# Contrast adjustment on one core: tiles of one size against tiles of two sizes in the same ring

## The chip, the core and the metric

The kernel runs on one core of a Trainium2 chip. Time is device time of that core in microseconds (us). The engines that matter here are VectorE (DVE in the profile), ScalarE (ACT), TensorE (PE, with PEld for its weight loads), GpSimd (POOL) and SyncE (SP). Transfers between the chip's main memory (DRAM) and the core's on-chip memory (SBUF, 128 partitions) are done by 16 DMA engines. They are fed from two hardware queues here: q1 holds what SP issues, which are all the loads, and q10 holds what ACT issues, which are all the stores.

## The reference

```python
def reference(x, factor):          # x: 16 x 3 x 512 x 512 float32, factor 1.5
    mean = np.mean(x, axis=(2, 3), keepdims=True)
    return np.clip(mean + factor * (x - mean), 0, 1).astype(np.float32)
```

There are 48 images (16 times 3) of 262,144 values each. Each image needs its own mean before its first output can be computed. With w = (1 - factor) / 262144, an output is clip(factor * x + w * sum(image), 0, 1). 50.33 MB come in and 50.33 MB go out.

## The kernel before

**Tiles.** The images are cut into rows of ROW = 8192 floats (32 KB), so an image is 32 rows. A tile is 128 rows, one per partition: four images, 4 MB. There are 12 tiles. They live in `ring` (L66), six slots of 32 KB per partition; tile t uses slot t % 6.

**Loads** (`load`, L68, issued on SP at L76). The order is written by hand (L103 to L112, a manual schedule: each engine's instructions run in program order, and the semaphores between engines follow from the data). Tile 0 is loaded in two pieces, 2048 columns and 6144 columns. Tile 1 is one load. Tiles 2 and 3 come in one load of 8 MB, tiles 4 and 5 in another. After `compute(t)` the load of tile t + 6 follows on SP; it waits until tile t has been stored, since it takes its slot.

**Compute** (`compute`, L78). VectorE sums columns 0 to SUM = 4352 of the tile per row (L81), while ScalarE sums the other 3840 columns with an accumulating copy into `junk` (L84). Two accumulating matmuls with `blockw` (L86 on ScalarE's sums, L87 on VectorE's) add the 32 rows of each image, multiply by w and put the result into every row of the image, in PSUM (`bias`). `blockw` is a 128 x 128 block diagonal matrix with 32 x 32 blocks of w, filled by GpSimd (L61, L63). Then VectorE makes two passes over the tile in place: multiply by factor and add the shift (L91), and clip (L94). ACT issues the store (L101). Tile 0 does this in two parts (`FIRST`, 2048 and 6144 columns), each with a store of its own. The other tiles do it in one.

**Queues.** On ACT the order is: sum of tile t, store of tile t, sum of tile t + 1, and so on. On VectorE: sum, pass, pass of tile t, then those of tile t + 1. On SP: the loads alone.

Of the kernel before, what the change touches and what calls it, by code (L numbers as in the profile page):

```python
# [1 line left out]

# [4 lines left out]


P = 128  # L10
ROW = 8192
BUFS = 6
SHORT = 2048
FIRST = (SHORT, ROW - SHORT)
SUM = 4352


@with_exitstack
def kernel(
    ctx: ExitStack,  # L20
    tc: tile.TileContext,
    x: bass.AP,
    factor: float,
    out: bass.AP,
):

    nc = tc.nc
    f32 = mybir.dt.float32  # L30
    Alu = mybir.AluOpType
    Act = mybir.ActivationFunctionType

    B, C, H, W = x.shape
    n_img, n_pix = B * C, H * W
    ppi = n_pix // ROW
    per_tile = P // ppi
    n_tiles = n_img // per_tile
    assert ppi * ROW == n_pix and per_tile * n_tiles == n_img

    factor = float(factor)
    wconst = (1.0 - factor) / float(n_pix)

    x_f = x.rearrange("b c h w -> (b c h w)")
    out_f = out.rearrange("b c h w -> (b c h w)")

    def dram(ap, t, c0=0, c1=ROW):
        return bass.AP(tensor=ap.tensor, offset=t * P * ROW + c0, ap=[[ROW, P], [1, c1 - c0]])

    consts = ctx.enter_context(tc.tile_pool(name="consts", bufs=1))  # L50
    xpool = ctx.enter_context(tc.tile_pool(name="xpool", bufs=1))
    small = ctx.enter_context(tc.tile_pool(name="small", bufs=1))
    psum = ctx.enter_context(tc.tile_pool(name="psum", bufs=1, space=bass.MemoryType.PSUM))


    sums = small.tile([P, 2 * n_tiles], f32, name="sums")
    junk = small.tile([P, ROW - SUM], f32, name="junk")
    bias = psum.tile([P, n_tiles], f32, name="bias")

    blockw = consts.tile([P, P], f32, name="blockw")  # L60
    nc.gpsimd.memset(blockw, 0.0)  # L61
    for a in range(0, P, ppi):
        nc.gpsimd.memset(blockw[a : a + ppi, a : a + ppi], wconst)  # L63


    ring = xpool.tile([P, BUFS, ROW], f32, name="ring")  # L66

    def load(t, c0=0, c1=ROW, n=1):  # L68

        b = t % BUFS  # L70
        src = bass.AP(
            tensor=x_f.tensor,
            offset=t * P * ROW + c0,
            ap=[[ROW, P], [P * ROW, n], [1, c1 - c0]],
        )
        nc.sync.dma_start(out=ring[:, b : b + n, c0:c1], in_=src)  # L76

    def compute(t):  # L78
        xt = ring[:, t % BUFS, :]
        own = sums[:, 2 * t : 2 * t + 2]  # L80
        nc.vector.tensor_reduce(  # L81
            out=own[:, 0:1], in_=xt[:, 0:SUM], axis=mybir.AxisListType.X, op=Alu.add
        )
        nc.scalar.activation(out=junk, in_=xt[:, SUM:ROW], func=Act.Copy, accum_out=own[:, 1:2])  # L84
        shift = bias[:, t : t + 1]
        nc.tensor.matmul(shift, blockw, own[:, 1:2], start=True, stop=False)  # L86
        nc.tensor.matmul(shift, blockw, own[:, 0:1], start=False, stop=True)  # L87
        c = 0
        for n in FIRST if t == 0 else [ROW]:
            part = xt[:, c : c + n]  # L90
            nc.vector.tensor_scalar(  # L91
                out=part, in0=part, scalar1=factor, scalar2=shift, op0=Alu.mult, op1=Alu.add
            )
            nc.vector.tensor_scalar(  # L94
                out=part, in0=part, scalar1=0.0, scalar2=1.0, op0=Alu.max, op1=Alu.min
            )
            store(t, c, c + n)
            c += n

    def store(t, c0, c1):  # L100
        nc.scalar.dma_start(out=dram(out_f, t, c0, c1), in_=ring[:, t % BUFS, c0:c1])  # L101

    with tc.manual_schedule():  # L103
        load(0, c1=SHORT)
        load(0, c0=SHORT)
        load(1)
        load(2, n=2)
        load(4, n=2)
        for t in range(n_tiles):
            compute(t)  # L110
            if t + BUFS < n_tiles:
                load(t + BUFS)  # L112


# [1 line left out]
_INS = ['x', 'factor']  # L116
_OUTS = [((16, 3, 512, 512), 'float32')]

_NUMBERS = {'factor': 1.5}


# [26 lines left out]
```

## Time and profile before

| what | value |
|---|---|
| median of 3 runs | 239.26 us (239.2 to 239.46) |
| span of the profiled execution | 237.3 us, 285 instructions |
| around the span, by the median | 2.0 us (the page gives the profiled execution no time of its own beside its span) |
| busy: DVE / ACT / PE | 163.1 (69%) / 43.2 (18%) / 14.1 (6%) us |
| moved | 100.66 MB, mean 424 GB/s over the span |
| transfers | 11 loads, 13 stores; all of 4 MB but two loads of 8 MB and the two pieces of tile 0 |
| time from the last load's landing to the last store's issue | 203.73 to 218.17 us |

The page divides the span into 40 slices of 5.93 us; a row of digits shows how busy an engine was in each, in tenths. A DMA share is the busy time of all 16 DMA engines as a share of 16 times the stretch, so share x 16 x stretch / packets is the mean time of one packet on its engine. A packet here is one contiguous piece of one partition's row: a 4 MB transfer is 128 packets of 32 KB, eight on each DMA engine. Very small packets (4 bytes) are the semaphore updates, 16 for each transfer. Shares a little over 100% come from packets that reach over the edge of the stretch.

### The profile page before, as it was taken

How to read it: one execution, taken by the hardware profiler on the slowest of the kernel's cores; microseconds unless marked ns; L12 is line 12 of the kernel's file. 1: busy time of each engine (PE TensorE's matmuls, PEld its weight loads, DVE VectorE, ACT ScalarE, POOL GpSimd, SP SyncE). 2: the span in 40 equal slices, each digit the busy share in tenths (PEclk: the TensorE clock that was granted, in tenths of full speed). 3: DMA queues.
4: the chain of work that ended last, by engine and by line, in shares of the span. 5: the costliest groups of instructions: out<-in, count | busy, mean ns of one | idle time of the engine just before them, and what ended most of it. 6: DMA issues, size and time to landing. Idle time of an engine off the chain costs nothing.

```text
span 237.3 us, 285 instructions
## 1 busy us (share of the span) xinstructions
PE 14.1 (6%) x48; PEld 12.0 (5%) x48; DVE 163.1 (69%) x38; ACT 43.2 (18%) x25; POOL 0.9 (0%) x9
## 2 busy tenths in 40 slices
PE   0010010001010001010010100100100100010000
PEld 0010010001010001010010100100100100010000
DVE  0079989048989328999989898891892795687000
ACT  2050230041050023050320504101400500500000
POOL 1000000000000000000000000000000000000000
DMA  7999999999999999999999999999999999999996
GB/s 297 410 442 442 421 442 359 456 439 441 442 436 414 403 431 442 442 442 442 436 442 436 414 409 425 442 442 442 442 436 442 436 420 403 425 442 442 442 442 265
DMA packets 3712, 100.66 MB, mean 424 GB/s; under 512 B 384, under 2 KB 384, under 8 KB 384
## 3 DMA queue, kind: packets, MB, share of 16 engines
q1 hardware_dynamic: 1840, 50.33, 49.7%
q10 hardware_dynamic: 1872, 50.33, 49.2%
HBM read 50.33 MB, written 50.33 MB: 424 GB/s over the span
## 4 chain that ended last, share of the span: by engine, by line
DMA 57%; DVE 29%; another core or an unknown queue 3%; PE 1%; SPq 1%; issue 0%; DVEq 0%
DMA ring<-in_x_dram 41%; DMA out_dram<-ring 16%; DVE sums L81 10%; DVE ring L91 9%; DVE ring L94 9%; PE bias L87 1%; SPq L76 1%; DVEq L91 0%
## 5 line engine op out<-in xcount | busy, mean ns | idle before, releaser
L81 DVE TENSOR_REDUCE sums<-ring 128x1 f32<-128x4352 f32 x12 | 56.2, 4683 | 45.7 <-DMA ring<-in_x_dram 45.7
L84 ACT ACTIVATE junk<-ring 128x3840 f32<-128x3840 f32 x12 | 40.8, 3403 | 163.3 <-DMA ring<-in_x_dram 107.5
L91 DVE TENSOR_SCALAR ring<-ring,bias 128x8192 f32<-128x8192 f32 (+2 forms) x13 | 54.1, 4163 | 8.9 <-PE bias L87 7.4
L94 DVE TENSOR_SCALAR ring<-ring 128x8192 f32<-128x8192 f32 (+2 forms) x13 | 53.3, 4099 | 0.4
L86 PE MATMUL bias<-sums,blockw 128*128 128x1 f32 x24 | 7.0, 361 | 190.8 <-ACT junk L84 190.8
L86 PEld LDWEIGHTS bias<-sums,blockw 128*128 128x128 f32 x24 | 6.0, 312 | 191.7 <-ACT junk L84 175.2
L87 PE MATMUL bias<-sums,blockw 128*128 128x1 f32 x24 | 7.0, 363 | 4.3 <-DVE sums L81 3.9
L87 PEld LDWEIGHTS bias<-sums,blockw 128*128 128x128 f32 x24 | 6.0, 311 | 5.3 <-DVE sums L81 5.0
L84 ACT ACTIVATION_READ_ACCUMULATOR junk<-ring 128x1 f32 x12 | 2.2, 186 | 0.0
L84 ACT ACT_TABLE_LOAD x1 | 1.3, 1283 | 0.7 <-PEq L129 0.7
L63 POOL MEMSET blockw<- 32x32 f32 x4 | 0.5, 117 | 0.2
L61 POOL MEMSET blockw<- 128x128 f32 x1 | 0.2, 204 | 0.3 <-POOLq L129 0.3
L129 POOL MEMSET const-bfloat16-1.0<- 128x1 bf16 x1 | 0.1, 111 | 0.0
L129 POOL MEMSET const-uint8-127<- 128x1 uint8 x1 | 0.1, 111 | 0.0
L129 POOL MEMSET const-float32-1.0<- 128x1 f32 x1 | 0.1, 108 | 0.0
L129 POOL MEMSET const-float32-0.0<- 128x1 f32 x1 | 0.1, 103 | 0.2 <-issue 0.2
## 6 DMA issues: line engine op xcount, KB each, us to landing
out_dram<-ring ACTq DMA_DIRECT2D x11, 4096.0 KB, 35.8
ring<-in_x_dram SPq DMA_DIRECT2D x7, 4096.0 KB, 49.7
ring<-in_x_dram SPq DMA_DIRECT2D x2, 8192.0 KB, 66.7
ring<-in_x_dram SPq DMA_DIRECT2D x1, 3072.0 KB, 11.7
out_dram<-ring ACTq DMA_DIRECT2D x1, 3072.0 KB, 28.2
ring<-in_x_dram SPq DMA_DIRECT2D x1, 1024.0 KB, 4.8
out_dram<-ring ACTq DMA_DIRECT2D x1, 1024.0 KB, 17.5
```

The lines of the kernel that those rows point to most:

```text
L61: nc.gpsimd.memset(blockw, 0.0)
L63: nc.gpsimd.memset(blockw[a : a + ppi, a : a + ppi], wconst)
L76: nc.sync.dma_start(out=ring[:, b : b + n, c0:c1], in_=src)
L81: nc.vector.tensor_reduce(out=own[:, 0:1], in_=xt[:, 0:SUM], axis=mybir.AxisListType.X, op=Alu.add)
L84: nc.scalar.activation(out=junk, in_=xt[:, SUM:ROW], func=Act.Copy, accum_out=own[:, 1:2])
L86: nc.tensor.matmul(shift, blockw, own[:, 1:2], start=True, stop=False)
L87: nc.tensor.matmul(shift, blockw, own[:, 0:1], start=False, stop=True)
L91: nc.vector.tensor_scalar(out=part, in0=part, scalar1=factor, scalar2=shift, op0=Alu.mult, op1=Alu.add)
L94: nc.vector.tensor_scalar(out=part, in0=part, scalar1=0.0, scalar2=1.0, op0=Alu.max, op1=Alu.min)
L129: nc = _bacc.Bacc("TRN2", target_bir_lowering=False, num_devices=1)
```

## The change

The ring stays 192 KB per partition, now as six units of 32 KB (`SLOTS`, `UNIT`). A list `PLAN` gives each tile its first unit and its width in units. Eight tiles replace twelve: tiles 0 and 1 of four images (one unit each, units 0 and 1), tiles 2 to 5 of eight images (two units each), tiles 6 and 7 of four images (units 4 and 5). In a tile of eight images a partition holds one contiguous row of 16384 floats (64 KB), so an image is 16 rows. In the DRAM tensors the rows of such a tile are 64 KB apart.

- Loads: tile 0 in two pieces as before, then tiles 1, 2, 3 without a wait. Tile 4 goes to units 0 and 1 and waits for the stores of tiles 0 and 1. Tile 5 goes to units 2 and 3 and waits for the store of tile 2. Tiles 6 and 7 go to units 4 and 5 and wait for the store of tile 3. There are 9 loads and 9 stores (tile 0 has two of each).
- Sums: VectorE takes VEC = 4480 columns per unit of width in one instruction (8960 in a wide tile); ScalarE takes 3712 columns per unit, in one instruction for a narrow tile and in two for a wide one. A wide tile has a matmul for each of ScalarE's two sums and one for VectorE's.
- The two passes over a wide tile are each one instruction over 16384 columns, and its store is one transfer of 8 MB.
- GpSimd makes two block matrices (16 x 16 and 32 x 32 blocks), each with a memset and two `affine_select` in place of the memsets of single blocks.

```diff
-ROW = 8192
-BUFS = 6
+UNIT = 8192
+SLOTS = 6
 SHORT = 2048
-SUM = 4352
+VEC = 4480
+PLAN = ((0, 1), (1, 1), (2, 2), (4, 2), (0, 2), (2, 2), (4, 1), (5, 1))
...
+    def dram(ap, t, c0, c1):
+        row = UNIT * PLAN[t][1]
+        return bass.AP(tensor=ap.tensor, offset=start[t] + c0, ap=[[row, P], [1, c1 - c0]])
...
-    blockw = consts.tile([P, P], f32, name="blockw")
-    nc.gpsimd.memset(blockw, 0.0)
-    for a in range(0, P, ppi):
-        nc.gpsimd.memset(blockw[a : a + ppi, a : a + ppi], wconst)
+    for w in sorted({w for _, w in PLAN}):
+        rows = n_pix // (UNIT * w)
+        m = consts.tile([P, P], f32, name=f"block{w}")
+        nc.gpsimd.memset(m, wconst)
...
+    def load(t, c0=0, c1=None):
+        c1 = UNIT * PLAN[t][1] if c1 is None else c1
+        nc.sync.dma_start(out=cols(t, c0, c1), in_=dram(x_f, t, c0, c1))
...
         nc.vector.tensor_reduce(
-            out=own[:, 0:1], in_=xt[:, 0:SUM], axis=mybir.AxisListType.X, op=Alu.add
+            out=own[:, 0:1], in_=cols(t, 0, VEC * w), axis=mybir.AxisListType.X, op=Alu.add
         )
-        nc.scalar.activation(out=junk, in_=xt[:, SUM:ROW], func=Act.Copy, accum_out=own[:, 1:2])
+        for i in range(w):
+            a = VEC * w + i * (UNIT - VEC)
+            nc.scalar.activation(
+                out=junk, in_=cols(t, a, a + UNIT - VEC), func=Act.Copy,
+                accum_out=own[:, 1 + i : 2 + i],
+            )
...
+    held, after = {}, {}
+    for t, (s, w) in enumerate(PLAN):
+        before = [held[k] for k in range(s, s + w) if k in held]
+        after.setdefault(max(before, default=-1), []).append(t)
+        held.update({k: t for k in range(s, s + w)})
 
     with tc.manual_schedule():
-        load(0, c1=SHORT)
-        load(0, c0=SHORT)
-        load(1)
-        load(2, n=2)
-        load(4, n=2)
-        for t in range(n_tiles):
+        load(0, 0, SHORT)
+        load(0, SHORT)
+        for t in after[-1][1:]:
+            load(t)
+        for t in range(len(PLAN)):
             compute(t)
-            if t + BUFS < n_tiles:
-                load(t + BUFS)
+            for n in after.get(t, ()):
+                load(n)
```

More of the change, by code (lines that the diff above doesn't have):

```diff
@@ L10 @@
 P = 128
-ROW = 8192
-BUFS = 6
+UNIT = 8192
+SLOTS = 6
 SHORT = 2048
-FIRST = (SHORT, ROW - SHORT)
-SUM = 4352
+VEC = 4480
+PLAN = ((0, 1), (1, 1), (2, 2), (4, 2), (0, 2), (2, 2), (4, 1), (5, 1))
 @with_exitstack
@@ L34 @@
     B, C, H, W = x.shape
[L35 to L39, printed above, removed]
+    n_pix = H * W
+    assert P * UNIT * sum(w for _, w in PLAN) == B * C * n_pix
     factor = float(factor)
@@ L45 @@
     out_f = out.rearrange("b c h w -> (b c h w)")
-    def dram(ap, t, c0=0, c1=ROW):
-        return bass.AP(tensor=ap.tensor, offset=t * P * ROW + c0, ap=[[ROW, P], [1, c1 - c0]])
+    start, begin = [], 0
+    for _, w in PLAN:
+        start.append(begin)
+        begin += P * UNIT * w
+    def dram(ap, t, c0, c1):
+        row = UNIT * PLAN[t][1]
+        return bass.AP(tensor=ap.tensor, offset=start[t] + c0, ap=[[row, P], [1, c1 - c0]])
     consts = ctx.enter_context(tc.tile_pool(name="consts", bufs=1))
@@ L53 @@
     psum = ctx.enter_context(tc.tile_pool(name="psum", bufs=1, space=bass.MemoryType.PSUM))
-    sums = small.tile([P, 2 * n_tiles], f32, name="sums")
-    junk = small.tile([P, ROW - SUM], f32, name="junk")
-    bias = psum.tile([P, n_tiles], f32, name="bias")
-    blockw = consts.tile([P, P], f32, name="blockw")
-    nc.gpsimd.memset(blockw, 0.0)
-    for a in range(0, P, ppi):
-        nc.gpsimd.memset(blockw[a : a + ppi, a : a + ppi], wconst)
-    ring = xpool.tile([P, BUFS, ROW], f32, name="ring")
@@ L68, in load @@
[L68 to L74, printed above, removed]
-        )
-        nc.sync.dma_start(out=ring[:, b : b + n, c0:c1], in_=src)
+    sums = small.tile([P, 3 * len(PLAN)], f32, name="sums")
+    junk = small.tile([P, UNIT - VEC], f32, name="junk")
+    bias = psum.tile([P, len(PLAN)], f32, name="bias")
+    block = {}
+    for w in sorted({w for _, w in PLAN}):
+        rows = n_pix // (UNIT * w)
+        m = consts.tile([P, P], f32, name=f"block{w}")
+        nc.gpsimd.memset(m, wconst)
+        v = m.rearrange("p (g j) -> p g j", j=rows)
+        nc.gpsimd.affine_select(
+            out=v, in_=v, pattern=[[-rows, P // rows], [0, rows]], compare_op=Alu.is_ge,
+            fill=0.0, base=0, channel_multiplier=1,
+        )
+        nc.gpsimd.affine_select(
+            out=v, in_=v, pattern=[[rows, P // rows], [0, rows]], compare_op=Alu.is_ge,
+            fill=0.0, base=rows - 1, channel_multiplier=-1,
+        )
+        block[w] = m
@@ L78, in compute, with cols, store @@
+    ring = xpool.tile([P, SLOTS * UNIT], f32, name="ring")
+    def cols(t, c0, c1):
+        a = PLAN[t][0] * UNIT
+        return ring[:, a + c0 : a + c1]
+    def load(t, c0=0, c1=None):
+        c1 = UNIT * PLAN[t][1] if c1 is None else c1
+        nc.sync.dma_start(out=cols(t, c0, c1), in_=dram(x_f, t, c0, c1))
+    def store(t, c0, c1):
+        nc.scalar.dma_start(out=dram(out_f, t, c0, c1), in_=cols(t, c0, c1))
     def compute(t):
-        xt = ring[:, t % BUFS, :]
-        own = sums[:, 2 * t : 2 * t + 2]
+        w = PLAN[t][1]
+        row = UNIT * w
+        own = sums[:, 3 * t : 3 * t + 3]
@@ L81, in compute @@
         nc.vector.tensor_reduce(
-            out=own[:, 0:1], in_=xt[:, 0:SUM], axis=mybir.AxisListType.X, op=Alu.add
+            out=own[:, 0:1], in_=cols(t, 0, VEC * w), axis=mybir.AxisListType.X, op=Alu.add
         )
-        nc.scalar.activation(out=junk, in_=xt[:, SUM:ROW], func=Act.Copy, accum_out=own[:, 1:2])
+        for i in range(w):
[3 more added lines that the diff above has]
+                accum_out=own[:, 1 + i : 2 + i],
+            )
@@ L85, in compute @@
         shift = bias[:, t : t + 1]
-        nc.tensor.matmul(shift, blockw, own[:, 1:2], start=True, stop=False)
-        nc.tensor.matmul(shift, blockw, own[:, 0:1], start=False, stop=True)
+        for i in range(w):
+            nc.tensor.matmul(shift, block[w], own[:, 1 + i : 2 + i], start=i == 0, stop=False)
+        nc.tensor.matmul(shift, block[w], own[:, 0:1], start=False, stop=True)
         c = 0
-        for n in FIRST if t == 0 else [ROW]:
-            part = xt[:, c : c + n]
+        for n in (SHORT, row - SHORT) if t == 0 else (row,):
+            part = cols(t, c, c + n)
@@ L98, in compute @@
             c += n
-    def store(t, c0, c1):
-        nc.scalar.dma_start(out=dram(out_f, t, c0, c1), in_=ring[:, t % BUFS, c0:c1])
-    with tc.manual_schedule():
-        load(0, c1=SHORT)
-        load(0, c0=SHORT)
-        load(1)
-        load(2, n=2)
-        load(4, n=2)
-        for t in range(n_tiles):
+    held, after = {}, {}
[3 more added lines that the diff above has]
+        held.update({k: t for k in range(s, s + w)})
+    with tc.manual_schedule():
+        load(0, 0, SHORT)
[3 more added lines that the diff above has]
+        for t in range(len(PLAN)):
             compute(t)
-            if t + BUFS < n_tiles:
-                load(t + BUFS)
+            for n in after.get(t, ()):
+                load(n)
 _INS = ['x', 'factor']
```

## The prediction

> **What bounds the kernel now.** I read the head of the page first: VectorE is busy 69% of the span, ScalarE 18%, and the DMA engines are at nine tenths or more in all slices but the first and the last. Then the busy time by stages, from the first packet (1.8 us) to the last (235.7):
>
> ```profile
> DVE  0079989048989328999989898891892795687000
> ...
> DMA  7999999999999999999999999999999999999996
> GB/s 297 410 442 442 421 442 359 456 439 441 442 436 414 403 431 442 442 442 442 436 442 436 414 409 425 442 442 442 442 436 442 436 420 403 425 442 442 442 442 265
> ```
> ```profile
> 56.00:203.70 147.70, 9.39 (x33) 8.02 (x32) 117.38 (x26) 27.97 (x16) 0.00 (x0) 1.00 1.00 433
> 203.70:235.70 32.00, 1.18 (x4) 1.01 (x4) 13.60 (x3) 3.50 (x2) 0.00 (x0) 1.00 0.99 426
> ```
>
> The last columns are PE clock, DMA share and GB/s. The DMA share is 1.00 from 56 to 203.7 and 0.99 after the last load. So the time is the work of the DMA engines, plus a start and an end. Next, what a packet costs: the DMA view in four stretches (24 KB loads alone, 5.4 to 11.7 us; 32 KB loads alone, 12.6 to 21.4; loads and stores together, 56.6 to 75; stores alone, 207.2 to 215.9). Columns are packets, MB, share of 16 engines.
>
> ```profile
> q1 hardware_dynamic: 112, 2.75, 101.3%
> ```
> ```profile
> q1 hardware_dynamic: 112, 3.67, 96.5%
> ```
> ```profile
> q1 hardware_dynamic: 128, 4.19, 52.7%
> q10 hardware_dynamic: 116, 3.80, 47.8%
> ```
> ```profile
> q10 hardware_dynamic: 112, 3.67, 97.6%
> ```
>
> A 24 KB packet: 1.013 x 16 x 6.3 / 112 = 0.912 us. A 32 KB load: 0.965 x 16 x 8.8 / 112 = 1.213; a 32 KB store: 0.976 x 16 x 8.7 / 112 = 1.213; mixed, 1.212 and 1.213. Direction and mixing make no difference. Two queues with work take turns, one packet each: 8 loads and 8 stores of 1.213 us are 19.4 us, and the last loads land 19.4 us apart (their sums start at 165.03, 184.40, 203.76).
>
> The span by this: the packet records give 0.309 us for 8 KB and 0.009 for a semaphore packet. Per engine 16 x 0.309 + 16 x 0.912 + 176 x 1.213 + 24 x 0.009 = 233.2 us. The first packet starts at 1.8, the last one ends 1.6 before the end, and slow packets at the start and near 37 us add 0.7: 237.3. The compute chain sets nothing in the middle; it would only if both queues ran dry. The dangerous place is the end:
>
> ```profile
> 203.76 4.69 DVE L81 TENSOR_REDUCE sums<-ring 128x1 f32<-128x4352 f32 x1 [4.98 <-DMA ring<-in_x_dram]
> ...
> 218.17 0.34 ACTq L101 DMA_DIRECT2D out_dram<-ring  x1
> ```
>
> After the last load, 14.4 us pass until its store is issued. The DMA engines then still have 32.0 us of work, of which the last store is 9.7. So 22.3 us of older stores cover 14.4 us of compute, with 7.9 to spare.
>
> **The change, part by part.** The sum goes against the 237.3 us span; the 2.0 us around it to the median of 239.26 stay.
>
> *Packets.* From 24 to 32 KB a packet grows by 0.301 us, so 32 KB is 1.204 for its bytes and 0.009 for being a packet (8 KB against 24 KB gives 3 x 0.309 - 0.912 = 0.015 for two, 0.008 each). A 64 KB packet should take 2 x 1.204 + 0.009 = 2.417 us against 2.426 for two. The four wide tiles replace 64 packets per engine in each direction by 32: 64 x 0.009 = 0.58 us saved. Six transfers fewer are six semaphore packets fewer: 0.05. Together **-0.63 us**. No trace row shows a 64 KB packet. If it is cut in two, the saving is 0.05; if its fixed part vanished wholly, 1.15.
>
> The Trainium skill ("SBUF — State Buffer", The DMA setup-cost knee) gives every transfer a fixed cost of about 2 us and advises the largest single transfer. By that, six transfers fewer would save an estimated 12 us. The trace disagrees: with transfers queued the share stays 1.00 across their borders, so I don't use it. Against the change, the page "DMA: Bandwidth & Descriptors" (Latency and other measured facts) says that copies slow down when partition rows lie 2 MiB apart or more in main memory, at 512 KiB not yet; here the pitch goes from 32 to 64 KiB, and no run here shows a large one.
>
> *Compute.* A narrow tile's sum grows to 4480 / 4352 x 4.69 = 4.82 us, hence 14.5 us from landing to store. A wide tile: sum at most 2 x 4.82 = 9.6; matmul and its waits 0.7; passes by the slope of the rows for 2048 and 8192 columns (1.29 and 4.49, 0.52 ns a column), 8.76 and 8.69. That is 27.8 us against 28.7 for two tiles before. ScalarE's two sums (2 x 3.3) and their matmuls end under VectorE's 9.6. All this hides behind the DMA engines as long as neither end of the ring starves.
>
> *GpSimd.* Two memsets (0.20 us each by the row of before) and four selects, which no row shows. The first matmul wants its block at 16.5 us and GpSimd is done at 1.6 before. The selects may take (16.5 - 1.6) / 4 = 3.7 us each without any effect; the nearest rows, memsets, take 0.1 to 0.2. Even if late, they would delay tile 0 alone, while the DMA engines have loads until about 69 us.
>
> *The new waits on SP.* Tile 4 needs both first tiles stored, tile 5 one wide store, tiles 6 and 7 another. Tiles 5 to 7 are queued behind tile 4. I walked one DMA engine with the rows above: turns of one packet, 1.213 or 2.417 us. Stored to next load's issue 0.6 us (tile 0's last packet, 55.4, to the load at 55.96). A queue that was empty starts between 1.0 us after issue (first load, 0.74 to 1.74) and 3.7 to 4.9 (first store, issued at 20.91 beside running loads); I take 3.7, the row with the other queue busy. Slowest engine's last packet and landing, 2.0 after the typical engine's.
>
> | tile | load lands | computed | stored |
> |---|---|---|---|
> | 2 | 45.4 | 73.1 | 114.2 |
> | 3 | 70.8 | 100.7 | 152.9 |
> | 4 | 123.5 | 151.2 | 184.4 |
> | 5 | 162.2 | 189.9 | 215.8 |
> | 6 | 188.8 | 204.3 | 225.5 |
> | 7 | 203.3 | 218.7 | 235.2 |
>
> Tiles 0 and 1 are stored at 70.7 and 80.4. Loads are issued at 81.0 (tile 4), 114.8 (5), 153.5 (6, 7). The load queue is empty from 69 to 85, which the store of tile 1 covers until 80.4; tile 2's store, issued at 73.1, takes over with 3.6 us to spare. At the end tile 7's store is issued 6.8 us before tile 6's store ends. No gap, so the sum is the packets alone: 237.3 - 0.6 = 236.7, and 239.26 - 0.6 = **238.7 us**. The stall that goes is none; the bound stays.
>
> **Rivals.**
> *A gap at the end (slower).* Turns are by packet, so a 64 KB store beside a 32 KB load takes two thirds of the engine. Tile 7's eight load packets need 9.7 us alone, but 8 x 3.63 = 29 us when tile 5's store runs beside all of them. In the walk tile 5's store comes late enough that they run nearly alone. If tile 4's load catches an earlier turn at 82 us, or queues start in 1.0 us, tile 5 is computed 2.5 us earlier, its store meets all of tile 7's load, and that lands at 213. Then 14.5 us of compute and 1.3 to the first packet stand against 225.5 - 213 = 12.5 us of work: a gap of 3.3. It decides from a landing at 209.7 on. Price 0 to 5 us; the middle of it, 2.6, gives 238.7 + 2.6 = 241.3. For it: the walk tips with 2 us of shift. Against it: the store queue's observed slow start, which lets tile 7 run alone. 0.18.
>
> *The rows are cut into two packets.* Then only 0.05 us is saved and turns stay even; the walk has no gap: 239.2. For it: no row of a 64 KB packet. Against: each contiguous row was one packet at 8, 24 and 32 KB. 0.14.
>
> *Long rows run slower per byte* (pitch, or uneven engines). The 32 wide packets each way are 64 x 2.42 = 155 us per engine; 1% more is 1.5 us: 240.2. Against it: the same 1.213 us in every pattern of before. 0.08.
>
> **Numbers.** Forecast 0.60, rivals 0.18, 0.14, 0.08. About 0.2% (0.48 us) is what a measurement of this kernel can tell from no change. The forecast's -0.63 lies just beyond, with some 0.2 of uncertainty: 0.43 faster, 0.17 same. Gap: 0.16 slower, 0.02 same. Cut rows: 0.13 same, 0.01 slower. Slow rows: 0.07 slower, 0.01 same. Faster 0.43, same 0.33, slower 0.24. The low end takes the vanished fixed part halfway, 238.3; the high end, 241.2, takes in cut rows, slow rows and half of the gaps.
>
> **What would show it.** the wide tiles' 64 packets per engine and direction becoming 32, that is 3328 data packets in all becoming 2304, with a wide packet near 2.417 us (right); the DMA share below 1.00 in a stretch between 75 and 85 or after 220 us (gap, wrong); tile 7's sum starting after 209.7 (the first rival); packets unchanged in number (the second); a wide packet over 2.43 us (the third).

## The result, and the profile after

| what | before | after |
|---|---|---|
| median | 239.22 us (239.04 to 239.46, 9 runs) | **243.27 us** (239.77 to 244.55, 9 runs) |
| profiled execution | 239.26 us (median), span 237.3 | 239.77 us, span 238.1 |

The ratio of after to before is 1.008, 95% interval 1.0056 to 1.0105: slower. (The ratio leaves out executions more than 1.5% above the fastest; here these are the longest of one continuous spread, so the ratio is milder than the medians' 1.017.) Forecast were 238.7 us and at most 241.2.

Two things differ, and they must be kept apart. The shortest execution is 0.5 us above before's median. And while all executions of before lie within 0.42 us, those of after lie within 4.8 us: 239.77, 239.77, 241.43, 241.63, 243.27, 243.83, 244.01, 244.06, 244.55. The profile fell on a shortest one. The same file run again gave 239.98 to 245.01, and its profile fell on the 245.01. So I read two traces of one kernel, **short** and **long**.

The heads of the pages, first of the short execution, then of the long one (digits and GB/s are slices of 5.95 and 6.08 us):

```profile
DVE  0088989698999899700008899807899989389300
...
DMA  7999999997999998999989898989979999989996
GB/s 300 405 440 440 461 508 396 396 474 319 418 463 440 529 352 352 462 418 440 440 352 529 352 529 352 529 352 440 518 341 462 402 424 496 440 352 440 440 440 264
DMA packets 2592, 100.66 MB, mean 423 GB/s; under 512 B 288, under 2 KB 288, under 8 KB 288
```
```profile
DMA  7999999999979999999989898989899999999792
GB/s 290 416 442 501 463 388 388 388 474 474 453 323 431 431 366 442 399 463 399 474 388 474 388 474 388 485 377 485 366 404 426 431 447 458 453 409 431 318 431 113
```

2592 packets less 288 semaphore updates are the 2304 data packets of the prediction (before: 3712 in all). So a wide row travels as one packet. The digits of short say that the DMA engines never stop, as forecast. In long the third slice from the end has 7, and the last slice 2 and 113 GB/s against 6 and 264: some engines still work while others are done.

What a wide packet costs, in a stretch of wide loads and stores alone (126 to 152 us, short):

```profile
q1 hardware_dynamic: 89, 5.83, 51.7%
q10 hardware_dynamic: 85, 5.57, 49.4%
```

0.517 x 16 x 26 / 89 = 2.417 us, the forecast's value.

The end, in the same stages as in the prediction, short and then long. The last three columns are PE clock, DMA share, GB/s:

```profile
56.00:208.03 152.03, 6.44 (x22) 5.50 (x22) 110.27 (x14) 23.72 (x14) 0.00 (x0) 1.00 1.01 434
208.03:236.70 28.67, 1.17 (x4) 1.00 (x4) 13.74 (x3) 3.39 (x2) 0.00 (x0) 1.00 0.93 402
```
```profile
213.30:227.00 13.70, 1.18 (x4) 1.01 (x4) 12.91 (x3) 3.39 (x2) 0.00 (x0) 1.00 0.90 390
227.00:229.00 2.00, 0.00 (x0) 0.00 (x0) 0.79 (x1) 0.00 (x0) 0.00 (x0) 1.00 0.80 344
229.00:236.50 7.50, 0.00 (x0) 0.00 (x0) 0.00 (x0) 0.00 (x0) 0.00 (x0) 1.00 0.98 419
236.50:242.00 5.50, 0.00 (x0) 0.00 (x0) 0.00 (x0) 0.00 (x0) 0.00 (x0) 1.00 0.36 155
```
```profile
208.03 4.82 DVE L98 TENSOR_REDUCE sums<-ring 128x1 f32<-128x4480 f32 x1 [3.81 <-DMA ring<-in_x_dram]
...
222.59 0.34 ACTq L92 DMA_DIRECT2D out_dram<-ring  x1
```
```profile
213.26 4.82 DVE L98 TENSOR_REDUCE sums<-ring 128x1 f32<-128x4480 f32 x1 [4.76 <-DMA ring<-in_x_dram]
...
227.82 0.34 ACTq L92 DMA_DIRECT2D out_dram<-ring  x1
```

Tile 7's landing to its store's issue takes 14.6 us in both (before: 14.4), but in long it begins 5.2 us later. Before the store is issued (227.82) the share falls to 0.80, and from 236.5 on it is 0.36: by the packet records twelve engines end at 238.4 to 238.6, the last four at 240.4 to 241.9.

Why the sum begins late is read from the packet records of the traces: 16 semaphore packets end a transfer, one from each DMA engine. In the table the first and last of the 16, in us:

| end of | short | long |
|---|---|---|
| store of tile 1 (units free for tile 4) | 80.5 to 80.9 | 80.6 to 80.9 |
| load of tile 4 | 122.6 to 125.5 | 123.2 to 126.7 |
| load of tile 5 | 161.3 to 161.7 | 161.9 to 166.0 |
| load of tile 6 | 187.9 to 188.3 | 188.5 to 192.6 |
| load of tile 7 | 207.2 to 207.7 | 200.6 to 212.9 |
| store of tile 7 | 236.2 to 236.7 | 238.4 to 241.9 |

In long the first engine has tile 7 6.6 us *earlier* than in short and the last one 5.2 us *later*: eleven engines end by 200.9, one at 204.7, four at 211.4 to 212.9. The sum waits for the last.

Up to 80.9 all engines are in step in both. Then both split at the same place. Tile 4's load is issued at 81.3 into a load queue that has been empty since 70.3:

```profile
81.34 0.33 SPq L89 DMA_DIRECT2D ring<-in_x_dram  x1
```

In short its first packets start at 85.5 to 85.7 on five engines and at 87.7 to 88.0 on the other eleven, one wide turn later, and take 3.1 to 3.9 us instead of 2.42. In long it is eleven engines at 85.5 to 86.0 and five at 89.2 to 89.8, with first packets of 2.7 to 3.5 us; the five send a store packet of 3.8 us before. In this stretch of short the engines are full, with few bytes for it:

```profile
85.40:91.50 6.10, 0.00 (x0) 0.00 (x0) 6.07 (x2) 0.00 (x0) 0.00 (x0) 1.00 1.05 376
```

That is 376 GB/s, against 434 from 56 to 208. In short the two groups are back in step by 161 us. In long they are not.

The accounts, per DMA engine, from the packet records ("slow" is packet time beyond 0.309, 0.912, 1.213 and 2.418 us for 8, 24, 32 and 64 KB; "idle" counts up to the last packet of the slowest engine, so an engine that is done early counts as idle):

| us | before | short | long |
|---|---|---|---|
| first packet starts | 1.7 | 1.8 | 1.8 |
| packets at their usual lengths | 233.2 | 232.7 | 232.7 |
| slow packets, mean of the engines | 1.3 | 2.3 | 4.0 |
| idle, mean of the engines | 0.0 | 0.0 | 3.4 |
| last packet of the slowest engine ends | 236.1 | 236.7 | 241.9 |
| span | 237.3 | 238.1 | 243.3 |

The forecast's saving is there (233.24 to 232.67, -0.57). Short pays 1.0 more than before for slow packets; at 85 to 90 alone lie 1.1. Long pays 2.8 more than before for slow packets and 3.4 for idle engines: about 1 us between 225 and 230, ahead of tile 7's store, and most of the rest after 238.4, while the last engines work on.

### The profile page after: what moved, and what is told of

Same layout as the page of the kernel before. It is cut to its first block, busy times and chain, and to the rows that moved or that the text cites. A ratio compares the mean times of both kernels' runs of the same rounds, so it can differ in the third digit from the quotient of the medians.

```text
span 238.1 us, 238 instructions
## 1 busy us (share of the span) xinstructions
PE 11.7 (5%) x40; PEld 10.0 (4%) x40; DVE 162.7 (68%) x26; ACT 42.0 (18%) x25; POOL 1.7 (1%) x10
## 2 busy tenths in 40 slices
DMA packets 2592, 100.66 MB, mean 423 GB/s; under 512 B 288, under 2 KB 288, under 8 KB 288
## 5 line engine op out<-in xcount | busy, mean ns | idle before, releaser
L98 DVE TENSOR_REDUCE sums<-ring 128x1 f32<-128x4480 f32 (+1 forms) x8 | 57.2, 7150 | 53.6 <-DMA ring<-in_x_dram 53.6
L103 ACT ACTIVATE junk<-ring 128x3712 f32<-128x3712 f32 x12 | 39.6, 3297 | 168.7 <-DMA ring<-in_x_dram 114.0
L114 DVE TENSOR_SCALAR ring<-ring,bias 128x16384 f32<-128x16384 f32 (+3 forms) x9 | 53.2, 5913 | 5.9 <-PE bias L110 5.2
L117 DVE TENSOR_SCALAR ring<-ring 128x16384 f32<-128x16384 f32 (+3 forms) x9 | 52.6, 5849 | 0.3
L109 PE MATMUL bias<-sums,block 128*128 128x1 f32 x24 | 7.0, 359 | 192.0 <-ACT junk L103 192.0
L109 PEld LDWEIGHTS bias<-sums,block 128*128 128x128 f32 x24 | 6.0, 310 | 192.9 <-ACT junk L103 161.8
L110 PE MATMUL bias<-sums,block 128*128 128x1 f32 x16 | 4.7, 362 | 9.8 <-DVE sums L98 9.8
L110 PEld LDWEIGHTS bias<-sums,block 128*128 128x128 f32 x16 | 4.0, 311 | 10.5 <-DVE sums L98 10.5
L75 POOL TENSOR_SCALAR_AFFINE_SELECT block<-block 128x128 f32<-128x128 f32 x2 | 0.6, 332 | 0.0
L71 POOL TENSOR_SCALAR_AFFINE_SELECT block<-block 128x128 f32<-128x128 f32 x2 | 0.6, 331 | 0.0
```

The source lines that it names most:

```text
L71: nc.gpsimd.affine_select(out=v, in_=v, pattern=[[-rows, P // rows], [0, rows]], compare_op=Alu.is_ge, fill=0.0, base=0, channel_multiplier=1,
L75: nc.gpsimd.affine_select(out=v, in_=v, pattern=[[rows, P // rows], [0, rows]], compare_op=Alu.is_ge, fill=0.0, base=rows - 1, channel_mul ...
L98: nc.vector.tensor_reduce(out=own[:, 0:1], in_=cols(t, 0, VEC * w), axis=mybir.AxisListType.X, op=Alu.add)
L103: nc.scalar.activation(out=junk, in_=cols(t, a, a + UNIT - VEC), func=Act.Copy, accum_out=own[:, 1 + i : 2 + i],)
L109: nc.tensor.matmul(shift, block[w], own[:, 1 + i : 2 + i], start=i == 0, stop=False)
L110: nc.tensor.matmul(shift, block[w], own[:, 0:1], start=False, stop=True)
```

## The experiments

Every kernel was timed beside the kernel before on the same chip. Ratios are to it, with 95% intervals. "Spread" is the time between the first and the last of the 16 engines at the end of the last load.

**Is the spread the kernel's own?** The kernel after, unedited.

> The changed kernel itself, unedited. Theory T (a gap at the end): the DMA engines wait for the last store in some executions and not in others, so its times spread, from 239.8 us with no gap to about 244 with one of 4 us; whenever a profiled span is over 239, the DMA queues hold no packet for the difference just before the last store, and tile 7's sum starts after 209.7 us. Rival S (long rows run slower, anywhere): a longer span comes with more 64 KB packets over 2.42 us spread over the middle, and no idle stretch at the end.

243.02 us (239.98 to 245.01, 10 runs), 1.0114 (1.0081 to 1.0148). Yes. Its profile is the long execution above.

**Does rival 1's gap exist?** This kernel leaves out tile 5's clip, so that its store goes early:

```diff
-            nc.vector.tensor_scalar(
-                out=part, in0=part, scalar1=0.0, scalar2=1.0, op0=Alu.max, op1=Alu.min
-            )
+            if t != 5:
+                nc.vector.tensor_scalar(
+                    out=part, in0=part, scalar1=0.0, scalar2=1.0, op0=Alu.max, op1=Alu.min
+                )
```

> The clip of tile 5 is left out, so its store is issued 8.7 us earlier; bytes and packets stay. T: the wide store now meets all of tile 7's load, which lands at 212 to 217 us; 14.5 us of compute follow against about 10 to 12 of store work: a gap of 2 to 6 us in every execution, 242 to 246 us. S: less work on VectorE and the same rows: the same 239.8 to 244 as the changed kernel, no later landing.

247.80 us (247.42 to 253.88, 4 runs), 1.0351 (1.0336 to 1.0366). Its last stage, in the timeline and by windows:

```profile
219.63 4.82 DVE L98 TENSOR_REDUCE sums<-ring 128x1 f32<-128x4480 f32 x1 [13.28 <-DMA ring<-in_x_dram]
...
234.18 0.34 ACTq L92 DMA_DIRECT2D out_dram<-ring  x1
```
```profile
220.00:226.00 6.00, 1.17 (x4) 1.00 (x4) 5.25 (x2) 3.07 (x2) 0.00 (x0) 1.00 1.00 431
226.00:236.00 10.00, 0.00 (x0) 0.00 (x0) 8.12 (x2) 0.00 (x0) 0.00 (x0) 1.00 0.20 85
```

Less VectorE work, a longer time. Tile 5's store is issued 8.0 us earlier (181.9), so its 64 KB packets run beside tile 7's 32 KB load packets and take two thirds of each engine. The two queues between 196 and 206 us:

```profile
q10 hardware_dynamic: 48, 3.15, 72.5%
q1 hardware_dynamic: 48, 1.57, 36.4%
```

Equal in packets, two to one in bytes: turns go by packet. (The Trainium skill, "DMA: Bandwidth & Descriptors", Queues, rings and completion order, says that an engine switches between queues only at packet borders; these rows agree.) Tile 7 lands at 219.6 in place of 208.0, tile 6 is stored by 227.7, and until 235.0, for 7.3 us, all 16 engines stand still. All are in step here (spread 0.6), so this gap needs no lateness. So the prediction's rival 1 is a mechanism that this kernel can show. Its price here is above the 0 to 5 us that I gave it, but the store is also moved by three times the 2.5 us that the rival assumed.

**Does the time of tile 5's store decide in the kernel after?** First the store is issued after ACT's sum of tile 6:

```diff
+        if late:
+            store(*late.pop())
...
-            store(t, c, c + n)
+            if t == 5:
+                late.append((t, c, c + n))
+            else:
+                store(t, c, c + n)
```

> Tile 5's store is issued on ACT only after ACT's sum of tile 6, about 3.9 us later; every packet stays. T: tile 7's load runs with fewer of tile 5's wide stores beside it, lands before 205 us, and no execution has a gap: all times within 0.5 us of 239.8, the long times are gone. S: the edit touches no row length, so times spread up to 244 as before the edit.

240.59 us (239.82 to 244.19, 7 runs), 1.0040 (1.0027 to 1.0053). It tells nothing: the store was issued at 189.90 (after: 189.84), one us after ACT's sum began (188.76) and before it ended. ACT didn't wait for its own sum to finish before it issued the transfer. So the store was held by data, behind a copy of the shift that the matmuls of tile 6 make:

```diff
+        if late:
+            nc.scalar.activation(out=junk[:, 0:1], in_=shift, func=Act.Copy)
+            store(*late.pop())
```

> The changed kernel with tile 5's store held on ACT until the matmuls of tile 6 are through (a copy of one column of the shift on ACT goes ahead of it), about 5.4 us later than unedited. Theory K with T (late engines find tile 5's wide store ready before they have finished tile 7's load, and that holds the load up): tile 7's load runs alone, lands before 204 us on all engines, no gap at the end; a gap of 0 to 3 us may open ahead of the held store. All times 239.8 to 242.5. Rival (the long times come from wide rows, wherever they run): up to 245 as unedited.

> The held store of tile 5 once more, one look. If this execution is a long one (over 241): K says that some engines are already 3 us or more late when tile 5's load ends at 161 us, and that lateness, not a held tile 7, makes the end; T says that tile 7's load lands after 209 us even so.

> The same kernel and the same expectations as late5b_2, in case that one falls on a short execution.

241.42 us (239.73 to 244.42, 12 runs), 1.0074 (1.0041 to 1.0108), and two more executions of 243.39 and 243.10. The store now leaves at 195.4 in the profiled short execution and at 198.9 and 198.6 in the two long ones, and there tile 7 lands at 197.3 to 201.6, far ahead of 209.7. Still they are long. So an early store of tile 5 isn't the cause of the length alone. In the first long one the engines are 4 us apart from tile 5's load on (161.3 to 165.3), with 64 KB packets 0.1 to 0.7 us slow at 163 to 179. The early engines run out of work while they wait for the held store (1.6 us per engine, a wait that the edit itself adds when tile 6 lands late), and the ends keep a part of the distance (238.6 to 240.3):

```profile
190.00:196.00 6.00, 0.24 (x2) 0.24 (x2) 6.00 (x2) 3.39 (x2) 0.00 (x0) 1.00 1.01 437
196.50:198.50 2.00, 0.28 (x2) 0.28 (x2) 1.66 (x1) 0.00 (x0) 0.00 (x0) 1.00 0.50 213
```

**Two narrow tiles in tile 5's place**, so that no wide store meets the last loads:

```diff
-PLAN = ((0, 1), (1, 1), (2, 2), (4, 2), (0, 2), (2, 2), (4, 1), (5, 1))
+PLAN = ((0, 1), (1, 1), (2, 2), (4, 2), (0, 2), (2, 1), (3, 1), (4, 1), (5, 1))
```

> Tile 5 becomes two tiles of four images, so four narrow tiles end the plan and the stores beside the last loads are 32 KB rows. T: turns at the end are even except beside tile 4's store, tile 8's load lands at 207 to 211 us, the gap is 0 to 1 us: 239.5 to 240.5 in every execution, 16 more packets per engine each way cost 0.1 us. S: three wide tiles in place of four: the extra time over 239.2 falls by a quarter and the spread stays, up to about 243.

245.37 us (240.08 to 247.16, 6 runs), 1.0056 (1.0038 to 1.0074; by the medians 1.026). Missed. The profile (span 245.4) has a spread of 8.8 (last load 209.5 to 218.3). Less wide work at the end, and a longer time.

**Do packets of two lengths do it?** The wide tiles stay, but their transfers are cut into two of 32 KB rows: stores only, loads only, both.

```diff
-            store(t, c, c + n)
+            for a in range(c, c + n, UNIT):
+                store(t, a, min(a + UNIT, c + n))
```

> Only the wide stores go out as two transfers of 32 KB rows; wide loads keep 64 KB rows. K: at the end, narrow loads meet narrow stores and the engines come back in step by half of the wide turn, so tile 7's load ends within 4 us on all engines: 239.0 to 240.5, little spread. G: as unedited, 240 to 245.

> Only the wide loads go out as two transfers of 32 KB rows; wide stores keep 64 KB rows. K: narrow loads meet wide stores over the whole middle, not only at the end, so the engines' ends of a load lie further apart than in the unedited kernel (over 5 us from tile 4 on) and the times reach 244 or more; the best execution about 239.5. G: as unedited, 240 to 245, with the engines' ends no further apart.

> Every wide load and store goes out as two transfers of 32 KB rows; tiles, sums and order stay. Theory K (engines fall out of step: beside each other, turns of 64 KB and of 32 KB carry the 16 DMA engines apart, and a transfer ends with its slowest engine): all packets are 32 KB again, the engines end tile 7's load within 2.5 us of each other, there is no gap: all times 239.0 to 239.8. Rival G (the wide tiles themselves: 8 MB to be stored and loaded before the next step): nothing of the waits changes, so the times still spread, 240 to 245.

| | median us (range, runs) | ratio | profiled span, spread |
|---|---|---|---|
| stores cut | 240.95 (240.48 to 241.72, 6) | 1.0067 (1.0050 to 1.0084) | 238.5, 1.8 |
| loads cut | 248.82 (244.63 to 257.90, 6) | 1.0221 (1.0200 to 1.0241; by the medians 1.040) | 243.0, 17.8 |
| both cut | 242.48 (239.65 to 242.87, 9) | 1.0110 (1.0077 to 1.0142) | 238.2, 1.4 |

Short load packets beside long store packets are by far the worst: the loads get a third of each engine (the two queues from 170 to 194 us below), and tile 7 lands on the engines between 194.9 and 212.7.

```profile
q10 hardware_dynamic: 96, 6.29, 69.5%
q1 hardware_dynamic: 96, 3.01, 30.8%
```

So unequal packets do drive the engines apart. But with all packets at 32 KB the time isn't back at 239 (and the profile fell on a short execution). This doesn't yet show a second thing at work in the kernel after: where loads are cut, tiles 2 and 3 also come in four loads of 4 MB, and that has a price of its own (next question). Another way to cut avoids it: eight unused columns between the ring's units, so that a wide transfer stays one transfer but goes as 32 KB packets.

```diff
-    ring = xpool.tile([P, SLOTS * UNIT], f32, name="ring")
+    ring = xpool.tile([P, SLOTS, UNIT + PAD], f32, name="ring")
```

> The changed kernel with 8 unused columns between the ring's units, so that a wide transfer stays one DMA of 8 MB but goes as packets of 32 KB, two for each row. Theory K (turns of 64 KB beside shorter ones carry the engines apart, and lengthen the store queue until the load queue runs empty at 70 us): 239.0 to 239.8 us in all executions, engines' ends of a load within 2 us of each other. Rival G (tiles of eight images and their waits): 240 to 245 as unedited.

241.53 us (239.66 to 242.70, 6 runs), 1.0092 (1.0060 to 1.0124); missed. Packet length alone is not the cause. In the profile (span 241.0, spread 5.9) the wide tiles' waits remain: the load queue runs empty at 120.

**What else did the change alter?** Twelve narrow tiles in the new code (`PLAN = tuple((i % 6, 1) for i in range(12))`): all sizes as before, the rest new.

> The new code with twelve tiles of one width: 12 single loads without the 8 MB pair, 4480 columns on VectorE, blocks made by selects. K and G alike: the time of the kernel before, 238.9 to 239.4 in all executions; anything beyond that would put part of the difference on the split of the sums, the block matrices or the plan's code.

241.09 us (240.34 to 241.79, 6 runs), 1.0065 (1.0043 to 1.0087). Above every expectation: something that I had counted as nothing costs 2 us. Besides the loop and the block matrices two things differ from before: VectorE's share, and that tiles 2 to 5 come in four loads of 4 MB rather than two of 8. Each of these two was put into the kernel before:

```diff
-SUM = 4352
+SUM = 4480
```

> The kernel before with one edit: VectorE sums 4480 columns of a tile, ScalarE 3712. Each tile's compute is 0.13 us longer. V: 240 to 241.8 us. P: 239.0 to 239.5 as before, since all of the compute hides.

239.39 us (238.96 to 239.78, 11 runs), 1.0006 (0.9997 to 1.0015): nothing.

```diff
-        load(2, n=2)
-        load(4, n=2)
+        load(2)
+        load(3)
+        load(4)
+        load(5)
```

> The kernel before with one edit: tiles 2 to 5 are loaded by four single loads of 4 MB in place of two of 8 MB. Theory P (the first loads' order sets which engine takes its turns late, and a late engine stays late to the end): the time of the narrow plan, 240 to 241.8 us, with one or two engines ending 2 us after the rest. Rival V (the split of the sums or the new block matrices moved the narrow plan): 239.0 to 239.5 as before.

241.98 us (241.03 to 243.61, 6 runs), 1.0122 (1.0095 to 1.0149). That is it, in the old kernel. The reverse, the new code with twelve narrow tiles and the paired loads:

> The narrow plan of the new code with the loads of tiles 2, 3 and 4, 5 paired into 8 MB as in the kernel before; sums and block matrices stay new. P: 239.0 to 239.5 us. V: 240.3 to 241.8 us as with the narrow plan.

239.32 us (239.06 to 239.63, 11 runs), 1.0001 (0.9992 to 1.0009). So the new loop, the block matrices, GpSimd's selects and the 4480 columns cost nothing, as forecast, and two first loads of 8 MB in place of four are worth 1.8 us here and 2.8 in the kernel before. The change itself keeps two such loads, tiles 2 and 3 with one 64 KB row per partition, and in both its traces all engines end them within 0.4 us (43.5 to 43.9, 69.9 to 70.3). So this price belongs to the narrow plan and to the kernels whose first loads are cut; that the kernel after pays it isn't shown. What it looks like, in the last us of the kernel before with four loads:

```profile
235.80:238.50 2.70, 0.00 (x0) 0.00 (x0) 0.00 (x0) 0.00 (x0) 0.00 (x0) 1.00 0.11 49
```

A share of 0.11 is two engines of 16. The other fourteen are done by 236.9, these two at 238.5. The distance between the first and the last engine grows from load to load, from 0.7 us at 34 to 1.9 at 90 and 4.1 at 208; in the kernel before it stays at 1.8 from 87 to 203. The same work, less evenly run.

**Can wide tiles win at all?** Six narrow tiles loaded in pairs as in the kernel before, then two wide and two narrow. `pair(t)` is one load of 8 MB for tiles t and t + 1, two rows of 32 KB per partition. Every first load is as before:

```diff
+PLAN = ((0, 1), (1, 1), (2, 1), (3, 1), (4, 1), (5, 1), (0, 2), (2, 2), (4, 1), (5, 1))
...
+        load(1)
+        pair(2)
+        pair(4)
```

> Ten tiles: six narrow ones loaded as in the kernel before (4 MB, 4 MB, two pairs of 8 MB), then two wide ones with 64 KB rows, then two narrow ones. The load queue never runs empty before the last load. If the empty queue at 70 us is what puts engines out of step: 238.8 to 239.6 us, no spread. If wide rows beside short ones do it wherever they stand: a spread from 239 up to 242 or more, engines' ends of the last load over 4 us apart in a long execution.

240.50 us (238.87 to 242.12, 6 runs), 1.0063 (1.0040 to 1.0086). The profiled execution is its 238.87, below all of before's: its engines end every load after 48 us within 0.3 us of each other, and the span is 237.2. Two wide tiles save 0.29 us of packets by the records, and here the engines keep step. The other five take 240.2 to 242.1. So the times spread without single first loads.

The expectation says that the load queue never runs empty before the last load. It does: it is empty from 114.7 us on, and tile 7, the second wide one, waits for tile 3's store:

```profile
120.13 0.34 SPq L95 DMA_DIRECT2D ring<-in_x_dram  x1
```

In this execution the restart cost nothing: its first packets start at 124.1 to 124.4 on all 16 engines and take 2.42 to 2.49 us.

**What starts the lateness?** In the first long execution with the held store, one engine ended tile 0's first short store (8 KB rows) at 44.0 and the others at 46.3 to 46.7. (In the long execution of the kernel after all 16 end it at 46.3 to 46.6, so there it can't be the seed.) If that store is the seed, tile 0 in one piece should end the spread:

```diff
-        for n in (SHORT, row - SHORT) if t == 0 else (row,):
+        for n in (row,):
```

> The kernel after with tile 0 summed, passed and stored in one piece; its two loads stay. Theory F (the short first stores of 8 KB rows are where one engine gets a turn out of step; in the long executions one engine ended the first short store at 44.0 us and the others at 46.3 to 46.7): without them no engine leaves the step, so all executions lie close together, 239.3 to 240.5 us, within 0.7 us of each other, and the ends of the last load lie within 1.5 us. Rival R (the load queue's restart at 81 to 88 us splits the engines by one wide turn whatever came before): the times stay spread from 239.8 up to 243 to 245 us, and tile 2's store ends at two times about 2.4 us apart. The compute chain of tile 0 ends about as early as before in one piece (passes 8.8 us after its sum and shift), so its later first store costs nothing while loads keep the engines busy to 69 us.

> The ten tiles (six narrow loaded in pairs as in the kernel before, two wide, two narrow) with tile 0 summed, passed and stored in one piece. F: the executions draw together at the low end, 238.6 to 239.2 us, below the kernel before by 0.1 to 0.6. R here: no load queue runs empty, so the restart cannot be the cause; if the spread of 238.9 to 242.1 us stays, it comes from wide rows beside short rows in the two queues, and the median stays near 240.5.

The kernel after with it: 243.43 us (240.81 to 244.43, 6 runs), 1.0122 (1.0078 to 1.0166). The ten tiles with it: 242.35 us (240.82 to 242.92, 6 runs), 1.0120 (1.0098 to 1.0141). Theory F falls: the times of both spread, and those of the ten tiles lie higher. In the first, tile 2's store ends at 115.8 on some engines and 118.3 on others, and the last load between 197.7 and 209.7, as rival R has it. In the ten tiles the load queue restarts as well, issued at 120.52: first packets at 125.7 to 126.6 that take 3.1 to 3.8 us, 1.3 us of engine time where the execution above paid none. Spans: 239.1 against 237.2. The last us of the first:

```profile
236.70:239.50 2.80, 0.00 (x0) 0.00 (x0) 0.00 (x0) 0.00 (x0) 0.00 (x0) 1.00 0.11 47
239.50:241.20 1.70, 0.00 (x0) 0.00 (x0) 0.00 (x0) 0.00 (x0) 0.00 (x0) 1.00 0.05 19
```

Two engines work on for 2.8 us, then one alone. No version beat the kernel before by its median.

All profiled executions, by span:

| kernel | spread, us | span, us |
|---|---|---|
| before, SUM 4480 | 0.4 | 237.1 |
| ten tiles, fast | 0.3 | 237.2 |
| before | 1.8 | 237.3 |
| narrow, paired | 1.9 | 237.6 |
| after, short | 0.4 | 238.1 |
| both cut | 1.4 | 238.2 |
| stores cut | 1.8 | 238.5 |
| ten tiles, tile 0 whole | 1.0 | 239.1 |
| narrow | 3.6 | 239.4 |
| before, four loads | 4.1 | 239.9 |
| padded ring | 5.9 | 241.0 |
| held store, two long ones | 4.0 and 4.1 | 241.4 and 241.7 |
| after, tile 0 whole | 12.0 | 242.5 |
| loads cut | 17.8 | 243.0 |
| after, long | 12.4 | 243.3 |
| two narrow for tile 5 | 8.8 | 245.4 |

Left out are the early store (0.6; 246.3), whose gap lies on all engines, and the two held or moved stores whose profiles were short (span 238.1). Otherwise the spans over 239.2 are those with a spread of 3.6 and more.

## Why the prediction was wrong

- **What bounds the kernel**: right in the main. Even in long, 232.7 of the 241.9 us up to the last packet are packets at their usual lengths.
- **Packets, -0.63 us**: right. 2.417 us a wide packet, 2304 data packets, -0.57 by the records. The rival of cut rows and the rival of slow long rows (as a price per byte) are out.
- **Compute, -0.9 us a wide tile; GpSimd, nothing**: right. 9.48 us for a wide sum, 0.33 us for a select, and the same time with the new code and narrow tiles (ratio 1.0001).
- **The walk**: within 2.4 us for the short execution up to tile 6 (tile 4 sum at 125.9 against 123.5, tile 5 at 162.1 against 162.2, tile 6 at 189.7 against 188.8), 4.7 us early for tile 7 (208.0 against 203.3). Of the 6.8 us to spare at tile 7's store, 4.4 were left (issued at 222.6, tile 6 stored at 227.0), and "no gap" held.
- **The step that failed: "I walked one DMA engine", with "Slowest engine's last packet and landing, 2.0 after the typical engine's."** There are 16, each taking its own turns, and a transfer has landed when the last of them is done. (The Trainium skill, "DMA: Bandwidth & Descriptors", Why a DMA increments its semaphore by 16 and not by 1, says the engines finish independently; the table of ends shows by how much here.) The distance is not a constant 2.0 but 0.3 to 17.8 us at the last load. It grows at the restart at 85 us and beside packets of unequal length, and with four first loads of 4 MB without either. In long it makes tile 7's sum start 5.2 us later than in short, with two costs: 1.7 us more of slow packets, and 3.4 us more of idle time, about 1 us ahead of tile 7's store and the rest while the last engines work on alone. Together they are 5.1 of the 5.2 us by which the slowest engine of long ends after that of short.
- **A second term, mis-sized**: the empty load queue's restart, for which the walk took 3.7 us of waiting, covered by stores, and no engine time. It took 4.2 to 6.6 us in short and 4.2 to 8.5 in long, with two groups of engines a turn or more apart, and the slow packets from 85 to 90 us cost 1.1 (short) and 1.3 us (long) of engine time. That alone outweighs the -0.57 and is as large as what short has over the forecast: 239.77 against 238.7.
- **The first loads**, priced by their bytes alone: in the kernel before, four loads of 4 MB in place of two of 8 cost 1.2%, so this isn't free in general. The change keeps two loads of 8 MB, and its engines are in step until 81 us; that it loses anything here isn't shown.
- **Rival 1**: mechanism shown by the early store, with a gap of 7.3 us on all engines. The tipping point held too: long has tile 7 landing at 213.3, past 209.7, and an idle stretch. But what tips it isn't the earlier store I named. In long that store is issued 4.3 us *later* than in short (first row short, second long):

```profile
189.84 0.34 ACTq L92 DMA_DIRECT2D out_dram<-ring  x1
```
```profile
194.12 0.34 ACTq L92 DMA_DIRECT2D out_dram<-ring  x1
```

  It meets tile 7's load even so, on the engines that come late out of tile 6's load (188.5 to 192.6). And with the store held, the lateness was there before tile 7 was loaded. So the rival's 241.3 lies nearer to the median than the forecast, but by another path than it named.

What is not settled: which event puts a given engine out of step, and whether the slow packets on late engines (some tenths of a us each) come from being out of step or make it. The first short store (tile 0 in one piece), the long packets (padded ring), the single first loads (ten tiles) and tile 5's early store (held store) have each been taken away in some kernel, and the times still spread. Of the kernels that spread, only those with cut first loads (both cut, narrow, before with four loads) have no restart of the load queue, so for it the question is open; what a restart costs differs between executions (1.1 and 1.3 us above, none and 1.3 in the two ten-tile traces). The spread was gone only with tiles of one size loaded in pairs (before, with either share of VectorE, and the new code with twelve narrow tiles); there neither queue runs empty in the middle either. That these causes add up is my reading, not shown.

## What to carry to other kernels

When the DMA engines are the bound, ask of a change not only how many packet-microseconds it saves but what keeps 16 engines in step: one packet length in all queues, queues that never run empty, waits that come early enough. Walk at least two engines that start one turn apart; if the plan has slack for one turn of the *largest* packet at the end and no more, it may tip in some executions. And run the unedited kernel often enough to see a spread before explaining a median; here one profile showed a kernel that was 0.5 us slower and another of the same file one that was 5.8 us slower.

## What the runs showed of the hardware beyond that

- Four loads of 4 MB in place of two of 8 MB, at the start and with no wait, lengthened the whole run by 1.2% (1.0095 to 1.0149), though the DMA share was 1.00 from 56 to 204 us and 0.99 from there to 236.
- ACT issued a transfer 1.1 us after the start of its own 3.3 us sum.
- A load into a queue that had run empty, beside a busy store queue, took 4 to 8.5 us to its first packets. In both traces of the kernel after and in the ten tiles with tile 0 whole these took 2.7 to 3.9 us in place of 2.42; in the fast execution of the ten tiles they took 2.42 to 2.49. The other queue's start can cost as much: with tile 0 in one piece the first store starts beside wide loads, and slow packets between 25 and 35 us make 1.9 us per engine.
- VectorE's sum over 8960 columns took 9.48 us, twice 4.82 less 0.16; a GpSimd select over 128 x 128 took 0.33 us.
